# Two layers of a hybrid trunk on one core: TensorE in source order through the mixers, attention units further apart

## The chip, the cores and the metric

The kernel runs on one core of a Trainium2 chip. The metric is device time in microseconds (us) for one execution of the whole program, the median of several runs. The profile is one execution, taken by the hardware profiler.

## The reference, cut to what matters

Two layers are run over 384 tokens: 128 context tokens and 256 denoising tokens, which share the weights. In each layer three token mixers work side by side on one normalised input, and a squared-ReLU MLP follows.

```python
def _layer(x, cond, P, l, ctx=None, tabs=None):
    ...
    h = _rms(x, P['norm1_g'][l]) * (1 + sc1) + sh1
    proj = h @ P['w_in'][l]
    u_conv, dq, dk, dv, cq, ckv, kpe, gl = jnp.split(proj, _split_points(), axis=-1)
    o_conv = _conv_module(u_conv, ...)          # depthwise convolution, 31 taps, 512 channels
    q = _rms(dq...); k = _rms(dk...)            # differential attention, 4 heads
    qm = _rms((rms(cq) @ P['w_uq'][l]), ...)    # latent attention, 8 heads
    km, vm = _mla_expand(ckv, kpe, P['w_ukv'][l], ...)
    ...
    od = _rms(_diff_attend(q, k, v, lam), P['diff_subln'][l]) * (1 - lam_init)
    o_diff = od.reshape(b, s, DIFF_W) @ P['w_diff_out'][l]
    o_mla = _mla_attend(qm, km, vm).reshape(b, s, MLA_W) @ P['w_mla_out'][l]
    gates = jax.nn.sigmoid(gl).reshape(b, s, N_BRANCH, D_MODEL)
    merged = gates[..., 0, :] * o_conv + gates[..., 1, :] * o_diff + gates[..., 2, :] * o_mla
    x = x + g1 * (merged @ P['w_out'][l])
    h = _rms(x, P['norm2_g'][l]) * (1 + sc2) + sh2
    x = x + g2 * (jnp.square(jax.nn.relu(h @ P['w_up'][l])) @ P['w_down'][l])
```

## The kernel before, in words

**Dense products.** Activations lie with channels on the 128 partitions and the 384 tokens along the columns. A product with a weight matrix goes in pieces of 128x1024 weights. SyncE's queue loads a piece (`raw`, L182), ScalarE rounds it into `wh` (L197), VectorE makes the rest `wl = wr - wh` (L198), and TensorE multiplies three times (`passes`, L204 to L206). This is the bulk of TensorE's work; such rows are called dense rows here. There are four buffers for `wr` and `wh` and three for `wl`.

**The mixers.** `mixers` runs three generators together through `weave` (L253). `dense` is the main one: projections to queries, keys and values (`qkv`), the compressed projections (`cproj`), the inputs of the convolution (`conv_in`), the expansions of the latent attention (`mla_q`, `mla_kv`), the gates and the output projections of the branches. Each of its steps reports how much TensorE work it was (1 is three dense rows of 384 columns). `chains` and `attention` are the sides. When a side yields a number it sleeps until that much dense work has been written out; these numbers stand in the table `W`. When it yields a name it sleeps until that flag is set. `tick` and `after` do the same for the delayed second half of a modulation unit (`mod_unit`, L360), the two transposes of L375.

**Attention.** `diff_attention` handles two heads (`c` is 0 or 1) in six units, `mla_attention` four heads (`g` is 0 or 1) in six units. A unit is: scores on TensorE (L753, L759); maxima on VectorE (L754, L760), their product with the scale (L762); exponentials on ScalarE (L766); on VectorE the normalisation, which is L810 to L812 in differential attention, and L967 and two rows of L969 (one for each head) in latent attention; then TensorE transposes the weights (L774 or L981), ScalarE copies them, and TensorE multiplies with the values (L821 or L996).

**The convolution** runs on VectorE: for each of four channel blocks 30 rows of L1071 on tile `z` (120 rows in a layer) and L349, which adds the squares up. `conv` (L1062) is written in the source only shortly before the last branch, but it depends only on `u` and on free `z` buffers. The sum of squares goes to TensorE (three products with ones, L327 with tile `z`), in `conv_norm`, after the first fourth of the output projection of latent attention.

**What sets the order.** The program is recorded in source order. A scheduler then decides the order on each engine: it takes the earliest recorded instruction that its own model thinks ready, and fills an engine that it thinks idle with later ones. That is how the rows of L1071 come between the attention's rows on VectorE, hundreds of rows ahead of their place in the source. The order that it finds is then fixed: on the chip each engine runs its own list from first to last, and waits at each entry for what that needs. `manual_schedule(engines=...)` makes the named engines keep the order of the source; the other engines are still ordered by the scheduler. Before, it is used only in `first_norm` (L1155).

Two places serve as marks below. **Mark A** is L327 with tile `z` in `cproj_norms` (called at L706): right behind the three pairs of L701, in the middle of the input projections. The first row of L1071 in a layer stands within three rows of L1071 of VectorE's answer to it. **Mark B** is L327 with tile `z` in `conv_norm`, near the end of the weave.

Of the kernel before, what the change touches and what calls it, by code (L numbers as in the profile page):

```python
# [36 lines left out]
ZTOK = (0, NP + PAD, 2 * NP + PAD)  # L37
# [93 lines left out]
PIECE = 1024  # L131


W = {"rm": 9, "rx": 8.5, "c0": 3.5, "c1": 2, "mh": 11, "qT": 12.5, "kT": 20, "s": 7, "od": 9, "mq": 7.5, "mk": 11.5, "ms": 9.5, "bc": 11}

NEAR = 2
ENGINES = {mybir.EngineType.PE, mybir.EngineType.Activation, mybir.EngineType.DVE}
# [9 lines left out]
class Body:  # L147
# [99 lines left out]
    def tick(self, w, due=False):  # L247
        for e in self.todo:
            e[0] -= w
        while self.todo and self.todo[0][0] <= (NEAR if due else 0):  # L250
            self.todo.pop(0)[1]()

    def weave(self, main, *sides):  # L253
# [65 lines left out]
        V.scalar_tensor_tensor(y, a, 1.875, y, ALU.add, ALU.mult)  # L319
        return y  # L320

    def rstd_bc(self, acc, toks, ahead=0):

        V = self.V
        st = self.psum("tr")
        for i, o in enumerate(toks):
            self.E.matmul(st[:, i : i + 1], acc[:, o : o + P], self.ones[:, :1], start=True, stop=True)  # L327
        v = self.tl(self.hp, [P, 4], "nwv", 2)
        dg = self.slot("tmp")
        with self.tc.high_priority(ahead):  # L330
            V.tensor_scalar(v[:, :NT], st[:, :NT], EPS, None, op0=ALU.add)
            y = self.rsqrt(v[:, :NT], NT)
            for i in range(NT):
                self.link = V.tensor_scalar(dg[:, i * P : (i + 1) * P], self.ident, y[:, i : i + 1], None,
                                            op0=ALU.mult)
        yield W["bc"]
        bc = self.psum("tr")
        self.E.matmul(bc[:, :T], self.ones, dg, start=True, stop=True)  # L338
        yield 1
        return bc  # L340
# [19 lines left out]
    def mod_unit(self, l, s, p, pool=None):  # L360

        V, E = self.V, self.E
        ps = self.psum("mm" if pool is None or p % 2 else "av")
        for h in range(2):
            w, _, n = self.raw((l, "mod", s, p, h), pool)
            for j in range(4):
                E.matmul(ps[32 * j : 32 * j + 32, :256], self.cond[:, 4 * h + j, :], w[:, j * 256 : j * 256 + 256],
                         start=h == 0, stop=h == 1, tile_position=(0, 32 * j))
        m = self.tl(pool, [P, 256], "m", 5) if pool else self.slot("tmpA", 256)
        self.A.copy(m, ps[:, :256])  # L370

        def rest():
            pt = self.psum("tr")
            for i in range(2):
                E.transpose(pt[:, i * P : i * P + P], m[:, i * P : i * P + P], self.ident)  # L375
            t = self.tl(self.cp, [P, 2, 2], "modt", 2)
            V.tensor_reduce(t, pt[:, : 2 * P].rearrange("p (i j c) -> p i c j", i=2, j=4)[:, :, 0:2, :], AX.X, ALU.add)
            b = self.mod_cols(s, p)
            o = PV["modb"][0]
            V.tensor_tensor(self.modT[l][:, b, :], t, self.pv[l][:, o + b.start : o + b.stop : b.step]  # L380
                            .unsqueeze(2).to_broadcast([P, 2, 2]), ALU.add)

        if pool:
            return rest
        self.after(4, rest)

    def mod_block(self, l, b):

# [399 lines left out]
        V.scalar_tensor_tensor(lo, pt[:, :T], gain, hi.bitcast(F32), ALU.mult, ALU.subtract)  # L788
        return hi, lo

    def diff_attention(self, c):
        V, A, E = self.V, self.A, self.E
        yield f"kT{c}"
        yield f"v{c}"
# [38 lines left out]


        e, last = scores(*units[0]), None
        yield W["s"]
        for i, u in enumerate(units):
            nxt = scores(*units[i + 1]) if i + 1 < len(units) else None
            wT = self.weightsT(e, P if u[0] == 0 else T)
            if last:  # L840
                values(*last)
            e, last = nxt, (*u, wT)
            yield W["s"]
        values(*last)
        y = self.rsqrt(ms, 2 * NT)
        for k in range(2):
# [71 lines left out]
    def mla_T(self, l, g):  # L918

        A, E = self.A, self.E  # L920
        m = self.m[g]
        yield f"mq{g}"
        if g == 1:
            yield "m0"
        yield W["mq"]
        qs = [self.tl(self.ap, [P, 2, T], "qT", 3) for _ in range(2)]
        for hh in range(4):
            pt = self.psum("tr")
            for tt in range(NT):
                E.transpose(pt[0:96, tt * P : tt * P + P], m["x4"][:, tt, hh, :], self.ident)  # L930
            A.activation(qs[hh // 2][0:96, hh % 2, :], pt[0:96, :T], AF.Identity,
                         scale=self.pv[l][0:96, PV["mq"][0] : PV["mq"][1]])
            if hh == 1:
                yield W["mh"]
        self.flags.add(f"mqT{g}")
        yield f"mk{g}"
        yield W["mk"]
        m["pairs"] = []
        for pr in range(2):
            kT = self.tl(self.ap, [P, 2, NK], "kT", 3)  # L940
            for i in range(2):
                hh = 2 * pr + i
                pt = self.psum("tr")
                for tt in range(4):
                    E.transpose(pt[0:96, tt * P : tt * P + P], m["ks"][tt // 2][:, tt % 2, hh, :], self.ident)  # L945
                A.activation(kT[0:96, i, :], pt[0:96, :], AF.Identity,
                             scale=self.pv[l][0:96, PV["mk"][0] : PV["mk"][1]])
            if pr == 0:
                yield W["mh"]
            m["pairs"].append((qs[pr], kT))  # L950
        self.flags.add(f"mkT{g}")

    def mla_attention(self, g):
        V, A, E = self.V, self.A, self.E
        yield f"mkT{g}"
        pairs, vm, qsc = (self.m[g][n] for n in ("pairs", "vm", "qsc"))
# [48 lines left out]


        es, last, done = scores(*units[0]), None, None
        yield W["ms"]
        for i, (pr, tt) in enumerate(units):
            if done is not None:  # L1010
                if g == 1:
# [6 lines left out]
                values(*last)  # L1018
                done = last[0] if last[1] else None
            last = (pr, tt, eT) if tt != 1 else None  # L1020
            yield W["ms"]
        values(*last)
        yield 2
        out(1)
# [51 lines left out]
    def conv_norm(self):  # L1076
        V, A = self.V, self.A
        yield "z"
        bc = yield from self.rstd_bc(self.zacc, ZTOK)
        for b in range(CB):  # L1080
            ch = self.slot("cq", T, F32R)
            cl = self.slot("cq", T, F32R)
            g = self.cgh[:, b : b + 1]
# [111 lines left out]
    def mixers(self, l):  # L1195
# [17 lines left out]
        self.d, self.m = [{}, {}], [{}, {}]  # L1213
        self.od, self.om, self.oc = [], [], []
        m = []
        self.weave(self.dense(l, h, m), self.chains(l), self.attention())
        ap.close()
        self.xs = ExitStack()
        self.xp = self.xs.enter_context(self.tc.tile_pool(name=f"xp{l}", bufs=1))
# [29 lines left out]
    def dense(self, l, h, m):  # L1249
# [21 lines left out]
        for i in range(4):  # L1271
            m += yield from self.gate(l, 1, i, h)
            yield from unit(1)
            if l > 0 and i == 0:
                yield from self.mla_kv(l, 0)
            if i == (1 if l == 0 else 2):
                yield from self.mla_q(l, 1)
            if i == (2 if l == 0 else 3):
                yield from self.mla_kv(l, 1)
        yield "od1"  # L1280
        for i in range(4):
            yield from self.branch_out(l, "od", i, self.od, m[2 * i : 2 * i + 2], None)
            yield from unit(1)
        self.flags.add("od")
        gm = []
# [19 lines left out]
            yield from self.mla_T(l, g)  # L1305
        yield from self.conv_norm()

    def attention(self):
        for c in range(2):
            yield from self.diff_attention(c)  # L1310
        for g in range(2):
            yield from self.mla_attention(g)

    def mlp(self, l):
        V, A = self.V, self.A
# [152 lines left out]
```

## Time and profile before

| | |
|---|---|
| median of 3 runs | 1357.85 us (1356.96 to 1357.92) |
| the profiled execution: its time, its span | 1356.93 us, 1355.2 us |
| TensorE products busy (records of matmuls) | 1330.5 us, 98% of the span, x8096 |
| TensorE weight loads busy | 1256.8 us, 93% |
| VectorE busy | 1067.6 us, 79%, x2549 |
| ScalarE busy | 684.9 us, 51% |
| mean granted TensorE clock over the span | 0.999 |
| layer 1's mixers, mark A to mark B | 825.57 to 984.52 us from the start |

Busy time is the time in which at least one record of the engine runs. TensorE's records overlap: consecutive dense rows of 384 columns start 0.17 us apart and each record is about 0.33 us long, so TensorE's work is better read from starts than from lengths. A wait shows as idle time in front of a row, with the row that ended it.

### The profile page before, as it was taken

The numbers are of one execution on the slowest core, as the hardware profiler recorded it, in microseconds if no ns is written. First come the engines' busy times: TensorE is split into PE (matmuls) and PEld (weight loads), VectorE is DVE, ScalarE is ACT, GpSimd is POOL, SyncE is SP. The second block draws the span as 40 slices with busy tenths as digits, with TensorE's granted clock in tenths as the row PEclk, the third lists the DMA queues.
The fourth block names the chain that finished last, engine by engine and source line by source line (L and its number), as shares of the span: only waits on it lengthen the run. The fifth ranks groups of instructions, "written<-read, shape, count | busy, mean of one in ns | idle before, by whom it ended". The sixth has DMA issues, their size and how long they took to land.

```text
span 1355.2 us, 21851 instructions
## 1 busy us (share of the span) xinstructions
PE 1330.5 (98%) x8096; PEld 1256.8 (93%) x8096; DVE 1067.6 (79%) x2549; ACT 684.9 (51%) x1297; POOL 16.7 (1%) x34
## 2 busy tenths in 40 slices
PE   5999999999999999999999999999999999999998
PEld 3989887789999999999999989878899999999998
DVE  6777999994998999975568789999999897435532
ACT  4555656453544662276335566565444466326621
POOL 0000000000000000000000000000000000000000
PEclk9999999999999999999999999999999999999999
DMA  9533344355574667754444333222358454333341
GB/s 367 180 92 113 109 156 147 127 209 194 162 255 128 206 217 247 250 169 125 148 148 141 90 95 109 84 91 82 124 177 256 142 190 151 125 125 126 125 148 54
DMA packets 62683, 209.46 MB, mean 155 GB/s; under 512 B 7840, under 2 KB 13600, under 8 KB 62320
## 3 DMA queue, kind: packets, MB, share of 16 engines
q1 hardware_dynamic: 56304, 196.93, 44.8%
q0 software_dynamic: 1808, 6.63, 1.5%
q10 hardware_dynamic: 4464, 4.50, 0.9%
q8 instruction: 64, 1.05, 0.3%
q14 instruction: 43, 0.35, 0.1%
HBM read 203.54 MB, written 4.49 MB: 154 GB/s over the span
## 4 chain that ended last, share of the span: by engine, by line
PE 74%; DVE 2%; ACT 1%; issue 0%; DVEq 0%
PE mm L204 15%; PE mm L206 15%; PE mm L205 15%; PE sc L204 8%; PE sc L206 8%; PE sc L205 8%; PE sc L759 1%; PE av L996 1%; PE tr L981 0%; PE av L821 0%; PE tr L338 0%; PE tr L945 0%; PE tr L327 0%; DVE wl L198 0%; DVE nm L760 0%; PE tr L774 0%
## 5 line engine op out<-in xcount | busy, mean ns | idle before, releaser
L197 ACT CAST wh<-wr 128x1024 fp32r<-128x1024 f32 (+3 forms) x280 | 290.0, 1036 | 333.8 <-PE mm L205 165.8
L198 DVE TENSOR_TENSOR wl<-wr,wh 128x1024 fp32r<-128x1024 f32 (+3 forms) x280 | 336.6, 1203 | 143.9 <-PE mm L206 51.6
L204 PE MATMUL mm<-h,wh 128*128 128x384 f32 x848 | 289.6, 341 | 0.5 <-ACT wh L197 0.5
L206 PE MATMUL mm<-h,wl 128*128 128x384 f32 x848 | 285.3, 336 | 0.5 <-DVE wl L198 0.5
L205 PE MATMUL mm<-h,wh 128*128 128x384 f32 x592 | 200.2, 338 | 0.5 <-DVE h L440 0.5
L204 PEld LDWEIGHTS mm<-h,wh 128*128 128x128 f32 x848 | 159.5, 188 | 5.8 <-issue 2.1
L206 PEld LDWEIGHTS mm<-h,wl 128*128 128x128 f32 x848 | 159.5, 188 | 1.8 <-DVE wl L198 1.0
L1071 DVE SCALAR_TENSOR_TENSOR z<-u,dwh,z 128x399 f32<-128x399 f32 x240 | 147.3, 628 | 0.5
L395 DVE SCALAR_TENSOR_TENSOR ot<-wm,srow 128x1024 bf16<-128x1024 f32 x112 | 136.6, 1220 | 4.0 <-DMA wm<-modwT 3.6
L205 PEld LDWEIGHTS mm<-h,wh 128*128 128x128 f32 x592 | 111.5, 188 | 1.6 <-DVE h L440 0.8
L204 PE MATMUL sc<-h,wh 128*128 128x384 f32 x336 | 112.5, 335 | 0.0
L206 PE MATMUL sc<-h,wl 128*128 128x384 f32 x336 | 112.4, 335 | 0.0
L205 PE MATMUL mm<-o,wh 128*128 128x384 f32 x320 | 107.8, 337 | 0.0
L204 PE MATMUL mm<-x,wh 128*128 128x386 f32 x288 | 98.1, 341 | 0.0
L206 PE MATMUL mm<-x,wl 128*128 128x386 f32 x288 | 97.5, 339 | 0.0
L205 PE MATMUL mm<-x,wh 128*128 128x386 f32 x288 | 97.5, 338 | 0.0
L204 PE MATMUL sc<-x,wh 128*128 128x386 f32 x272 | 92.5, 340 | 0.0
L206 PE MATMUL sc<-x,wl 128*128 128x386 f32 x272 | 92.1, 338 | 0.0
L205 PE MATMUL sc<-x,wh 128*128 128x386 f32 x272 | 92.1, 338 | 0.0
L1349 ACT ACTIVATE tmp<-tmp 128x128 f32<-128x128 f32 (+1 forms) x128 | 51.6, 449 | 69.2 <-DVE tmp L1347 69.0
L204 PE MATMUL mm<-wh,h 128*128 128x256 f32 (+1 forms) x288 | 83.8, 291 | 0.0
L206 PE MATMUL mm<-wh,h 128*128 128x256 f32 (+1 forms) x288 | 82.2, 286 | 0.0
(271 smaller groups left out, 2612.5 us busy)
## 6 DMA issues: line engine op xcount, KB each, us to landing
wr<-wts SPq DMA_DIRECT2D x306, 512.0 KB, 3.5
wm<-modwT SPq DMA_DIRECT2D x56, 512.0 KB, 4.4
srow<-condrow POOLq DMA_DIRECT2D x2, 1024.0 KB, 8.7
wr<-wts SPq DMA_DIRECT2D x4, 432.0 KB, 3.4
G<-xT SPq DMA_DIRECT2D x8, 192.0 KB, 4.3
wr<-wts SPq DMA_DIRECT2D x4, 384.0 KB, 3.1
G<-xT POOLq DMA_DIRECT2D x8, 192.0 KB, 3.3
xd<-G ACTq DMA_DIRECT2D x8, 192.0 KB, 2.6
```

What stands on the lines that cost most here:

```text
L197: self.A.copy(hi[:, :n], w[:, :n])
L198: self.V.tensor_tensor(lo[:, :n], w[:, :n], hi[:, :n].bitcast(F32), ALU.subtract)
L204: self.E.matmul(ps, ah, bh, start=start, stop=False)
L205: self.E.matmul(ps, ah, bl, start=False, stop=False)
L206: self.E.matmul(ps, al, bh, start=False, stop=stop)
L395: V.scalar_tensor_tensor(j, w, 0.5, self.srow[:, c, :], ALU.mult, ALU.mult, accum_out=self.modT[l][:, b, c : c + 1])
L759: E.matmul(sc[:, :n], q[c][:, qs], k[c][:, ks], start=True, stop=True)
L996: E.matmul(av[64 * i : 64 * i + 64, q0 : q0 + w], vm[:, (j + 1) if tt else 0, hv : hv + 64], eT[i][:, j * w : j * w + w], start=j == 0, st ...
L1071: self.V.scalar_tensor_tensor(z[b], self.u[:, b, k : k + ZW], self.dw[:, b * CK + k : b * CK + k + 1], z[b], ALU.mult, ALU.add)
L1349: A.activation(r[:, s:e], r[:, s:e], AF.Relu, bias=r[:, T + c : T + c + 1])
```

## The change

`mixers` records the weave under `manual_schedule` for TensorE. So within the weave TensorE runs exactly what the source writes, in that order; VectorE, ScalarE and GpSimd are still ordered by the scheduler. Most sleeping times in `W` are longer, some by layer: units of differential attention 10.2 and 9.2 instead of 7, of latent attention 10.5 and 7.6 instead of 9.5, the keys of latent attention 20 instead of 11.5, the transposes of outputs 14 instead of 9. `mla_kv` of the second group moves from among the gates to the output projections of differential attention. The second half of a modulation unit is due after 14 instead of 4.

```diff
-W = {"rm": 9, "rx": 8.5, "c0": 3.5, "c1": 2, "mh": 11, "qT": 12.5, "kT": 20, "s": 7, "od": 9, "mq": 7.5, "mk": 11.5, "ms": 9.5, "bc": 11}
+W = {"rm": 9, "rx": 8.5, "c0": 3.5, "c1": 2, "mh": 3, "qT": 12.5, "kT": 20, "s": (10.2, 9.2), "od": 14, "mq": (14, 1), "mk": 20, "ms": (10.5, 7.6), "bc": 11, "zc": 16}
...
-        while self.todo and self.todo[0][0] <= (NEAR if due else 0):
+        while self.todo and self.todo[0][0] <= (7 if due else 0):
...
-        yield W["bc"]
+        yield W[wait]
...
-        self.after(4, rest)
+        self.after(14, rest)
...
-        yield W["s"]
+        yield W["s"][l]
...
-        bc = yield from self.rstd_bc(self.zacc, ZTOK)
+        bc = yield from self.rstd_bc(self.zacc, ZTOK, wait="zc")
...
-        self.weave(self.dense(l, h, m), self.chains(l), self.attention())
+        with self.tc.manual_schedule(engines={mybir.EngineType.PE}):
+            self.weave(self.dense(l, h, m), self.chains(l), self.attention(l))
...
-            if i == (2 if l == 0 else 3):
-                yield from self.mla_kv(l, 1)
         yield "od1"
         for i in range(4):
             yield from self.branch_out(l, "od", i, self.od, m[2 * i : 2 * i + 2], None)
+            if i == l:
+                yield from self.mla_kv(l, 1)
```

How the instructions move, at two places of layer 1. The first is TensorE at mark A. Tile `sc` holds scores, `e` the weights of a unit, `z` a sum of squares, `mm` dense products. Before:

```order
L204 MATMUL mm_9427<-h_8135,wh_9431 128x384
L205 MATMUL mm_9427<-h_8136,wh_9431 128x384
L206 MATMUL mm_9427<-h_8135,wl_9432 128x384
L701 MATMUL tr_9474<-ones_99,z_9093 128x1 x3
L327 MATMUL tr_9480<-ones_99,z_9094 128x1 x3
L204 MATMUL mm_9428<-h_8108,wh_9431 128x384
L205 MATMUL mm_9428<-h_8109,wh_9431 128x384
L206 MATMUL mm_9428<-h_8108,wl_9432 128x384
```

And now:

```order
L204 MATMUL mm_9359<-h_8138,wh_9363 128x384
L205 MATMUL mm_9359<-h_8139,wh_9363 128x384
L206 MATMUL mm_9359<-h_8138,wl_9364 128x384
L701 MATMUL tr_9379<-ones_99,z_9056 128x1 x3
L327 MATMUL tr_9385<-ones_99,z_9057 128x1 x3
L759 MATMUL sc_9410<-kT_9069,qT_8829 128x128
L759 MATMUL sc_9413<-kT_9069,qT_8829 128x128
L774 MATMUL tr_9425<-ident_94,e_9328 128x128
```

The scores behind the mark belong to the second unit of the second half of differential attention, the transpose to its first. Before, the scores of five of those six units stood ahead of the mark; now one does. The same holds in layer 0.

The second place is VectorE late in layer 1's latent attention, second group (`e` the weights, `mr` their factors, `nm` maxima, the rows of L1071 the convolution, `wl` the rest of a weight piece, L349 the last sum of squares). Before, from the sixth and last unit of the group on:

```order
L967 RECIPROCAL mr_11038<-ms_2330_11025 128x2
L1071 SCALAR_TENSOR_TENSOR z_11171<-u_102,dwh_7853,z_11171 128x399
L969 TENSOR_SCALAR e_11034<-e_11034,mr_11038 128x384
L969 TENSOR_SCALAR e_11036<-e_11036,mr_11038 128x384
L198 TENSOR_TENSOR wl_11312<-wr_11309,wh_11311 128x1024
L1071 SCALAR_TENSOR_TENSOR z_11171<-u_102,dwh_7853,z_11171 128x399 x6
L198 TENSOR_TENSOR wl_11348<-wr_11345,wh_11347 128x1024
L1071 SCALAR_TENSOR_TENSOR z_11171<-u_102,dwh_7853,z_11171 128x399 x3
L1002 TENSOR_TENSOR o_11143<-av_11042,o_11142 128x384
L1071 SCALAR_TENSOR_TENSOR z_11171<-u_102,dwh_7853,z_11171 128x399 x3
L198 TENSOR_TENSOR wl_11408<-wr_11405,wh_11407 128x1024
L1071 SCALAR_TENSOR_TENSOR z_11171<-u_102,dwh_7853,z_11171 128x399
```

And now, from the third unit of the group on:

```order
L967 RECIPROCAL mr_10882<-ms_2287_10869 128x2
L969 TENSOR_SCALAR e_10878<-e_10878,mr_10882 128x384
L969 TENSOR_SCALAR e_10880<-e_10880,mr_10882 128x384
L349 TENSOR_TENSOR z_11177<-z_11177,tmpA_11309 128x399
L754 TENSOR_REDUCE nm_10927<-sc_10928 128x2
L762 TENSOR_TENSOR nm_10927<-nm_10927,qsc_10266 128x2
L198 TENSOR_TENSOR wl_11092<-wr_11089,wh_11091 128x1024
L967 RECIPROCAL mr_10937<-ms_2300_10926 128x2
L969 TENSOR_SCALAR e_10933<-e_10933,mr_10937 128x128
L969 TENSOR_SCALAR e_10935<-e_10935,mr_10937 128x128
L760 TENSOR_REDUCE nm_10986<-sc_10987 128x1
L760 TENSOR_REDUCE nm_10986<-sc_10990 128x1
```

Before, 13 rows of the convolution come after the group's last unit; now all 120 are over before its third unit, and no row of L1071 follows.

## Rows read from the trace of the kernel before

**Rows 1.** The page: busy time, share of the span, instructions of each engine
```profile
PE 1330.5 (98%) x8096; PEld 1256.8 (93%) x8096; DVE 1067.6 (79%) x2549; ACT 684.9 (51%) x1297; POOL 16.7 (1%) x34
```

**Rows 2.** Windows: us, busy us PE, PEld, DVE, ACT, POOL; granted clock; DMA share, GB/s
```profile
77.70:145.90 68.20, 67.44 (x457) 59.80 (x457) 52.69 (x163) 43.24 (x108) 0.00 (x0) 1.00 0.29 92
145.90:334.30 188.40, 185.27 (x1186) 156.47 (x1184) 163.46 (x467) 98.91 (x215) 1.10 (x2) 1.00 0.48 164
756.60:824.80 68.20, 67.43 (x457) 59.78 (x456) 52.65 (x162) 43.23 (x108) 0.00 (x0) 1.00 0.31 92
824.80:984.70 159.90, 157.87 (x922) 140.01 (x921) 155.58 (x416) 91.19 (x200) 0.55 (x1) 1.00 0.32 103
```

**Rows 3.** Waits of VectorE, layer 1, 824.8 to 984.7 us
```profile
DVE wl L198 <- PE mm L206: 1.6, 5, 0.6
...
DVE oms L592 <- ACT tmpA L591: 0.2, 1, 0.2
```

**Rows 4.** Waits of VectorE, layer 0, 145.9 to 334.3 us
```profile
DVE wl L198 <- ACT wh L197: 6.8, 4, 3.9
```

**Rows 5.** Waits of TensorE, whole span: what waited, for what, us, times, longest
```profile
PE tr L375 <- ACT tmpA L370: 2.1, 1, 2.1
...
PE tr L774 <- DVE e L812: 1.3, 2, 0.6
```

**Rows 6.** VectorE in time, layer 1, third unit of the second latent group
```profile
943.26 1.01 DVE L760 TENSOR_REDUCE nm<-sc 128x1 f32<-128x384 f32 x2
...
945.81 1.23 DVE L198 TENSOR_TENSOR wl<-wr,wh 128x1024 fp32r<-128x1024 f32 x1 [0.38 <-PE mm L206]
946.95 1.18 DVE L1071 SCALAR_TENSOR_TENSOR z<-u,dwh,z 128x399 f32<-128x399 f32 x2
948.04 0.16 DVE L967 RECIPROCAL mr<-ms 128x2 f32<-128x2 f32 x1
...
948.68 0.74 DVE L969 TENSOR_SCALAR e<-e,mr 128x384 f32<-128x384 f32 x2
```

**Rows 7.** TensorE in time, the transposes of the same unit
```profile
949.24 0.85 PE L981 MATMUL tr<-ident,e 128*128 128x128 f32 x6
```

**Rows 8.** Layer 0, second unit of the second latent group: TensorE's transposes
```profile
268.05 0.55 PE L981 MATMUL tr<-ident,e 128*128 128x128 f32 x3 [0.25 <-DVE e L969]
```

**Rows 9.** Chain of waits, 821 to 824 us: a dense row, then one attention unit
```profile
821.21 0.17 PE mm L205
...
821.56 0.84 PE sc L759 x4
822.40 0.48 PE tr L774 x3
822.88 0.67 PE av L821 x6
```

**Rows 10.** TensorE in time, marks A and B of both layers: start us, us
```profile
146.63 0.81 PE L327 MATMUL tr<-ones,z 128*128 128x1 f32 x6
...
334.13 0.72 PE L327 MATMUL tr<-ones,z 128*128 128x1 f32 x6
...
825.57 0.81 PE L327 MATMUL tr<-ones,z 128*128 128x1 f32 x6
...
984.52 0.72 PE L327 MATMUL tr<-ones,z 128*128 128x1 f32 x6
```

**Rows 11.** VectorE in time: the normalisation of one differential unit
```profile
820.62 0.16 DVE L810 RECIPROCAL ra<-s 128x1 f32<-128x1 f32 x1 [0.49 <-ACT e L766]
...
821.07 0.62 DVE L812 SCALAR_TENSOR_TENSOR e<-e,ra,e 128x384 f32<-128x384 f32 x1
```

**Rows 12.** Groups of TensorE: a modulation unit's products (busy us, records)
```profile
L367 PE MATMUL mm<-wr,cond 128*32 128x256 f32 x256 | 19.4, 402 | 0.9 <-DMA wr<-wts 0.9
```

**Rows 13.** Windows near the start; the column behind POOL is the granted clock
```profile
20.00:23.30 3.30, 1.96 (x20) 0.79 (x20) 1.61 (x6) 2.27 (x5) 0.00 (x0) 1.00 1.02 420
23.30:26.80 3.50, 3.00 (x10) 2.54 (x10) 3.20 (x7) 0.89 (x2) 0.00 (x0) 0.51 1.03 424
```

More of the change, by code (lines that the diff above doesn't have):

```diff
@@ L320, in rsqrt, with rstd_bc @@
         return y
-    def rstd_bc(self, acc, toks, ahead=0):
+    def rstd_bc(self, acc, toks, ahead=0, wait="bc"):
         V = self.V
@@ L789, in to_fm, with diff_attention @@
         return hi, lo
-    def diff_attention(self, c):
+    def diff_attention(self, l, c):
         V, A, E = self.V, self.A, self.E
@@ L842, in diff_attention @@
             e, last = nxt, (*u, wT)
-            yield W["s"]
+            yield W["s"][l]
         values(*last)
@@ L924, in mla_T @@
             yield "m0"
-        yield W["mq"]
+        yield W["mq"][g]
         qs = [self.tl(self.ap, [P, 2, T], "qT", 3) for _ in range(2)]
@@ L951, in mla_T, with mla_attention @@
         self.flags.add(f"mkT{g}")
-    def mla_attention(self, g):
+    def mla_attention(self, l, g):
         V, A, E = self.V, self.A, self.E
@@ L1007, in mla_attention @@
         es, last, done = scores(*units[0]), None, None
-        yield W["ms"]
+        yield W["ms"][l]
         for i, (pr, tt) in enumerate(units):
@@ L1020, in mla_attention @@
             last = (pr, tt, eT) if tt != 1 else None
-            yield W["ms"]
+            yield W["ms"][l]
         values(*last)
@@ L1306, in chains, with attention @@
         yield from self.conv_norm()
-    def attention(self):
+    def attention(self, l):
         for c in range(2):
-            yield from self.diff_attention(c)
+            yield from self.diff_attention(l, c)
         for g in range(2):
-            yield from self.mla_attention(g)
+            yield from self.mla_attention(l, g)
     def mlp(self, l):
```

## The prediction

> **What bounds the kernel now.** The page first [rows 1]: TensorE has a record running in 98% of the span, VectorE in 79%. That makes it a TensorE kernel, but both are averages, and the change touches the mixers alone, so I read the mixers by stretches, cut at mark A [rows 2]. Ahead of mark A VectorE is busy 52.7 of 68.2 us in both layers: there is room. Behind it, where the convolution starts, it is busy 155.6 of 159.9 us in layer 1 and 163.5 of 188.4 in layer 0. Then VectorE's waits. In layer 1 behind mark A there are five groups from 1.6 to 0.2 us, 3.0 together [rows 3]: VectorE runs through its list there practically without a pause. In layer 0 it also waits 6.8 us for pieces that ScalarE rounds late [rows 4]. TensorE's own waits in the mixers look small, from 2.1 us down [rows 5].
>
> So in layer 1, and less so in layer 0, there are two full engines side by side. Who leads is seen at one unit. In layer 1 VectorE starts the two rows of L969 that finish the third unit of the second latent group at 948.68 [rows 6]; the first is done after some 0.4 us, and TensorE starts that unit's transposes at 949.24 [rows 7]. In layer 0 TensorE waits 0.25 us in front of the transposes of the second unit for the same line [rows 8]. TensorE arrives within a few tenths of VectorE: the old order on VectorE just fits TensorE's pace. What matters is then how much work each engine has between mark A and such a unit, in either order.
>
> **What the change does to TensorE alone.** No product goes and none comes. A differential unit in one go takes 0.84 us of scores, 0.48 of three transposes (0.16 each) and 0.67 of six value records (0.22 for a pair) [rows 9]. By the order, three score pairs on 384 keys and one on 128, eight transposes and five value pairs cross mark A in each layer: 3 x 0.84 + 0.42 + 8 x 0.16 + 5 x 0.22 = 5.3 us. So mark A comes 5.3 us earlier and the stretch behind it gets 5.3 longer. Counting TensorE's rows at their start-to-start paces (0.17 for a dense row of 384, 0.11 for a plain transpose, and so on) I get 66.2 us for the first stretch of a layer, and 179.1 and 153.7 from mark A to mark B, of 68.2 [rows 2] and of 187.5 and 159.0 us [rows 10]: TensorE loses 2.0, 8.4, 2.0 and 5.3, together 17.7 us. That is all a better order of TensorE could return. I take 1.0 us of each 2.0 ahead of mark A as won, since units there get more room.
>
> **What it does to VectorE.** VectorE is not held to the source; the scheduler ordered it anew around the slower TensorE that it saw, and filled with convolution. I count VectorE's rows from its answer to mark A (L331) to the L969 row of one unit, old order against new, with the times from one start to the next of [rows 6]: L1071 1.09/2 = 0.545 us, L198 1.14, L760 0.47 (half of the pair's 1.01, less the overlap with the row behind); one differential unit's L810 to L812 0.93, which is 0.45 from the first start to the last and 0.48 of the last's 0.62 [rows 11].
>
> Layer 1, third unit of the second latent group: 35 more rows of L1071 (84 to 119) = 19.1; 8 more L760 = 3.7; three differential normalisations = 2.7; one L198 = 1.1; small rows 1.1. Sum **27.7 us** more. TensorE has, up to the same unit, 21 more dense rows (3.6 us, at 0.17 [rows 9]) and the 5.3: about 9 us. VectorE was even with it; now it is some 19 us late.
>
> Layer 0, second unit of the second latent group: 33 more L1071 (86 to 119) = 18.0; 8 L760 = 3.7; four normalisations = 3.7; three L198 = 3.4; five gate rows (L1114, taken like L760) = 2.3; some 30 small rows, among them layer constants that moved, = 3.0. Sum **34.1 us**. TensorE has 57 more dense rows (9.7), the 5.3 and two modulation units (1.4 each: 19.4/16 us of products [rows 12] and two transposes of 0.1): about 18 us, so VectorE is some 16 us late.
>
> TensorE now runs its list strictly. Behind a transpose that waits for its L969 row stand all later dense rows, and ScalarE's copies, the values and the next scores hang on it. The wait can no longer be filled.
>
> **The sum, mark A to mark B.** Layer 1: the transposes started 949.24 - 825.57 = 123.7 us behind mark A [rows 7, 10]; now 123.7 + 27.7 = 151.4. From there to mark B it was 984.52 - 949.24 = 35.3; 21 dense rows fewer (-3.6) and one small score pair more (+0.4) leave 32.1. Together 183.5 against 159.0: +24.5. Mark A comes 5.3 + 1.0 earlier: **+18.2 us**.
>
> Layer 0: 268.05 - 146.63 = 121.4 [rows 8, 10], plus 34.1 = 155.5. The rest was 334.13 - 268.05 = 66.1; 57 dense rows fewer (-9.7), two modulation units (-2.8), one score pair (+0.4), the 2.1 us wait of L375 gone (its second half is due later; -2.1) and some 1.0 of other waits: 50.9. Together 206.4 against 187.5, +18.9, less 6.3: +12.6. About 5 us of VectorE's wait for ScalarE's pieces [rows 4] lie ahead of that unit; with VectorE the late engine the rounding may be ready in time. Without them +7.6. I take the middle, **+10 us**.
>
> Edits with no price: the moved `mla_kv` and its weight piece (one load more or less late among SP's; transfers take 29 to 48% of the DMA engines' time in these stretches, the last column but one of [rows 2]); the later second halves of modulation units, whose results are needed hundreds of us later; `W["zc"]`, the longer sleep in `conv_norm` ahead of the broadcast behind mark B, where some 43 dense rows gave cover already. If VectorE's cover for the last went, the few us of `conv_norm` would come on top. Nothing behind mark B moves.
>
> 1356.93 + 18.2 + 10 = 1385.1 for the profiled execution; the median of the runs is 0.9 above it. I give **1385 us**, slower by 2.0%. Bounds of the terms: layer 0 +6.3 to +12.6, layer 1 +16.2 (if 2.0 more of the old losses vanish) to +18.2, and on top what a late TensorE does to VectorE: its gate rows and maxima wait for TensorE in turn, which the trace does not show; from 0 to the 6.8 us of the largest such row [rows 4].
>
> **Rivals.**
>
> *TensorE keeps its pace (9%).* The convolution rows that moved ahead lie in pauses of VectorE that open only because TensorE is ahead, so no L969 row is late; the 17.7 us come back and it ends at 1340, or at 1349 if half of it does. For it: TensorE's waits on VectorE in the old trace are tiny [rows 5]. Against: VectorE pauses 3.0 us in 159.9 [rows 3]; 35 rows of 0.545 us don't fit. It decides at some 5 us: if VectorE reaches that unit less than 5 us late in each layer, the gains ahead of mark A pay for it.
>
> *A wash (4%).* Layer 0 wins its 8.4 and 2.0, since its VectorE has 25 us to spare in all [rows 2], and layer 1 loses half of the 18: within 3 us of 1358.
>
> *The clock falls too (15%).* At the start there are 3.3 us in which TensorE works 1.96, and in the next 3.5 the granted clock is 0.51, the 1.2 GHz level; ten products take those 3.5 us, 0.35 each instead of 0.17 [rows 13]. Were lateness to pile up in waits of 2 to 4 us, say at the keys of each latent group (four places), each could cost some 1.7 us, 7 in all: 1392. Against: most waits would be about one us. The Trainium skill ("TensorE: Matmul & The Clock Gate", section on HAM oscillation) says that an idle TensorE falls back to half its clock and that a kernel which waits at each step pays for it again and again. By it this rival would be the rule; the mixers of this trace have no wait long enough to tell.
>
> *Forecast (72%)*: late by VectorE's list, at full clock.
>
> **The numbers.** A measurement of this kernel tells about 0.2% (2.7 us) from no change. Slower: forecast and falling clock, 87%; same 4%; faster 9%. The range for 8 in 10 leaves out the first two rivals (13%) and some 5% above. Below it takes in half of layer 1's and the low end of layer 0's term (9 + 6 = 15, less what I may have wrong in the 5.3: 1366); above, 12.6 + 18.2 + 6.8 + the clock's 7 = 44.6 would be 1402, not all of which comes at once: 1398.
>
> **What would show it.** TensorE's waits for L969 and L812 in front of L981 and L774 grow from 2 us to over 20, about a third of it in layer 0; mark A in layer 1 lies at some 158.95 + 24 us before mark B; the last row of L1071 in layer 1 ends more than 25 us ahead of mark B, and VectorE then idles; TensorE's busy share falls to 96 or 97%. A first stretch of 62 us confirms the small term. I am wrong in the mechanism if mark A to mark B in layer 1 stays under 165 us, or if TensorE waits mainly for ScalarE or for weight pieces; wrong in size if the waits for VectorE come out over 35 us.

## The result and the profile after

The changed kernel takes 1398.34 us, median of four runs (1397.82 to 1401.50), against 1357.79: a ratio of 1.0299, 95% interval 1.0286 to 1.0313. It is slower by 40.5 us. The forecast was 1385, and its range ended at 1398. The profiled execution took 1398.51 us with a span of 1396.7. The page, as in [rows 1]:

```profile
PE 1338.3 (96%) x8096; PEld 1264.9 (91%) x8096; DVE 1068.4 (76%) x2549; ACT 687.7 (49%) x1297; POOL 16.7 (1%) x34
```

The work is the same on every engine; only the shares fell. TensorE in time, marks A and B of both layers, as in [rows 10]:

```profile
145.16 0.58 PE L327 MATMUL tr<-ones,z 128*128 128x1 f32 x4
...
347.18 0.61 PE L327 MATMUL tr<-ones,z 128*128 128x1 f32 x5
...
835.45 0.70 PE L327 MATMUL tr<-ones,z 128*128 128x1 f32 x5
...
1026.22 0.61 PE L327 MATMUL tr<-ones,z 128*128 128x1 f32 x5
```

A third place, S, is the row L205 in `first_norm` in front of which TensorE is idle for 0.48 us. Before, then in the changed kernel:

```profile
41.90 0.44 PE L205 MATMUL mm<-h,wh 128*128 128x384 f32 x1 [0.48 <-DVE h L440]
```

```profile
43.27 0.44 PE L205 MATMUL mm<-h,wh 128*128 128x384 f32 x1 [0.48 <-DVE h L440]
```

Up to S the rows of TensorE, VectorE and ScalarE are the same in the same order in every trace of this case, and still S comes anywhere from 41.0 to 44.6 us. So I count what differs ahead of S as no effect of an edit, in a column of its own. Differences of these starts, beside those of before and of the runs that follow, tell where the time went (us; the last column runs from mark B of layer 1 to the end):

| | to S | S to A, layer 0 | A to B, layer 0 | B to A, layer 1 | A to B, layer 1 | rest |
|---|---|---|---|---|---|---|
| before | 41.9 | 104.7 | 187.5 | 491.4 | 159.0 | 370.6 |
| changed | 43.3 | 101.9 | 202.0 | 488.3 | 190.8 | 370.4 |
| e1 order alone | 44.0 | 110.5 | 225.5 | 498.4 | 188.6 | 372.5 |
| e2 table alone | 41.2 | 98.1 | 190.1 | 484.6 | 169.4 | 365.6 |
| e5 no convolution | 41.0 | 103.3 | 192.6 | 486.8 | 168.9 | 370.5 |
| e6 spread | 43.0 | 101.8 | 201.6 | 488.3 | 186.1 | 370.5 |
| e7 filled waits | 41.6 | 101.9 | 201.9 | 488.3 | 189.4 | 370.4 |
| e12 precedence | 41.6 | 98.4 | 201.3 | 485.2 | 187.9 | 370.4 |
| e9 both | 44.6 | 98.5 | 195.6 | 485.2 | 181.8 | 370.4 |
| e13 keys too | 41.1 | 98.4 | 194.9 | 485.2 | 178.9 | 370.4 |
| e14 no convolution, precedence | 41.1 | 98.5 | 190.3 | 485.2 | 170.0 | 370.5 |

The change lost 14.5 us behind mark A of layer 0 and 31.8 behind that of layer 1, and won 2.8 and 3.2 ahead of them; 1.4 us more went by ahead of S. TensorE's waits over the whole span, as in [rows 5]:

```profile
PE tr L945 <- DVE tok L912: 11.1, 4, 3.7
...
PE tr L774 <- DVE e L812: 9.5, 5, 3.4
PE tr L981 <- DVE e L969: 8.2, 8, 2.0
```

So it waits mainly for three rows of VectorE: the last one in making the keys of latent attention (L912), and the normalisations of the two kinds of units. Before, the one for L812 was 1.3 us. Windows, with the columns of [rows 2]: first one of the old trace, from mark A of layer 1 to the transposes of the third unit of the second latent group.

```profile
825.57:949.24 123.67, 121.64 (x705) 107.31 (x704) 121.06 (x351) 72.84 (x163) 0.00 (x0) 1.00 0.29 91
```

The changed kernel: both stretches ahead of mark A, then layer 1 from mark A to that same unit, then on to mark B.

```profile
76.96:145.16 68.20, 64.54 (x447) 60.61 (x446) 45.63 (x135) 38.56 (x88) 0.00 (x0) 0.97 0.31 100
...
767.25:835.45 68.20, 65.46 (x454) 61.61 (x452) 47.76 (x143) 39.65 (x92) 0.00 (x0) 0.97 0.33 96
835.45:994.03 158.58, 139.33 (x755) 120.01 (x755) 149.56 (x411) 82.82 (x185) 0.00 (x0) 0.94 0.24 78
994.03:1026.22 32.19, 32.19 (x193) 28.49 (x194) 14.60 (x29) 15.26 (x34) 0.55 (x1) 1.00 0.39 140
```

To that unit VectorE has 28.5 us more work than before (149.56 less 121.06), and it pauses 9.0 us in place of 2.6. TensorE's granted clock is 0.94 there. Behind that unit TensorE is busy without a gap, and VectorE works 14.6 of 32.2 us. VectorE's waits up to that unit, the counterpart of [rows 3]:

```profile
DVE nm L760 <- PE sc L759: 2.8, 5, 0.7
DVE nm L754 <- PE sc L753: 1.5, 2, 1.2
DVE wl L198 <- PE mm L206: 1.5, 5, 0.7
```

The pauses are new ones: VectorE now waits for scores, which stand behind waiting transposes in TensorE's list. There the two engines delay each other in turn. Not so in layer 0, from mark A to the transposes of the second unit of the second latent group (before, then changed):

```profile
146.63:268.05 121.42, 120.65 (x766) 100.23 (x766) 114.86 (x353) 68.26 (x158) 0.55 (x1) 1.00 0.41 136
```

```profile
145.16:295.28 150.12, 136.72 (x891) 112.89 (x890) 146.73 (x440) 79.42 (x185) 0.56 (x1) 1.00 0.42 137
```

VectorE has 31.9 us more work up to that unit, but its pauses shrank, from 6.6 to 3.4 us.

What a unit looks like inside: VectorE at that third unit, whose scores TensorE gave at 987.36 to 988.74.

```profile
988.21 0.56 DVE L760 TENSOR_REDUCE nm<-sc 128x1 f32<-128x384 f32 x1
988.68 0.62 DVE L1071 SCALAR_TENSOR_TENSOR z<-u,dwh,z 128x399 f32<-128x399 f32 x1
989.22 0.55 DVE L760 TENSOR_REDUCE nm<-sc 128x1 f32<-128x384 f32 x1
989.69 0.62 DVE L1071 SCALAR_TENSOR_TENSOR z<-u,dwh,z 128x399 f32<-128x399 f32 x1
990.49 1.23 DVE L198 TENSOR_TENSOR wl<-wr,wh 128x1024 fp32r<-128x1024 f32 x1 [0.17 <-PE mm L206]
991.63 0.15 DVE L762 TENSOR_TENSOR nm<-nm,qsc 128x2 f32<-128x2 f32 x1
991.70 1.30 DVE L1071 SCALAR_TENSOR_TENSOR z<-u,dwh,z 128x399 f32<-128x399 f32 x2
993.27 0.17 DVE L967 RECIPROCAL mr<-ms 128x2 f32<-128x2 f32 x1 [0.27 <-ACT e L766]
993.47 0.75 DVE L969 TENSOR_SCALAR e<-e,mr 128x384 f32<-128x384 f32 x2
```

From the first maximum to L969 it takes 5.3 us. Between the unit's own rows stand four rows of the convolution and a weight piece. The row of 0.15 us that ScalarE's exponentials need (L762) comes 1.9 us behind the second maximum. TensorE has 21 dense rows in the meantime, and then waits 0.98 us. The profile puts that wait down to L348 of ScalarE, which ends in the same tenth; the transposes start 0.56 us behind the start of L969, as they did before [rows 6, 7], so I count it as a wait for L969.

The same holds where VectorE has time to spare, ahead of mark A of layer 0. There ScalarE ended the exponentials of a differential unit at 104.0:

```profile
103.74 0.96 DVE L634 TENSOR_TENSOR tok<-tok,nwy 128x768 f32<-128x768 f32 x1
104.62 1.22 DVE L198 TENSOR_TENSOR wl<-wr,wh 128x1024 fp32r<-128x1024 f32 x1
105.75 0.42 DVE L636 TENSOR_TENSOR tok<-tok,row 128x256 f32<-128x256 f32 x1
...
107.90 1.22 DVE L198 TENSOR_TENSOR wl<-wr,wh 128x1024 fp32r<-128x1024 f32 x1
109.04 0.41 DVE L585 TENSOR_TENSOR tok<-tok,tmp 128x256 f32<-128x256 f32 x1
109.37 0.15 DVE L810 RECIPROCAL ra<-s 128x1 f32<-128x1 f32 x1
...
110.43 0.60 DVE L812 SCALAR_TENSOR_TENSOR e<-e,ra,e 128x384 f32<-128x384 f32 x1
```

And TensorE:

```profile
111.18 0.66 PE L774 MATMUL tr<-ident,e 128*128 128x128 f32 x2 [3.42 <-DVE e L812]
```

L810 could start at 104 and starts at 109.4, behind rows that make the next keys and two weight pieces. TensorE's old list had dense rows where it now waits 3.4 us.

### The profile page after: what moved, and what is told of

It is laid out like the page before. It is cut to its first block, busy times and chain, and to the rows that moved or that the text cites. A ratio compares the mean times of both kernels' runs of the same rounds, so it can differ in the third digit from the quotient of the medians.

```text
span 1396.7 us, 21854 instructions
## 1 busy us (share of the span) xinstructions
PE 1338.3 (96%) x8096; PEld 1264.9 (91%) x8096; DVE 1068.4 (76%) x2549; ACT 687.7 (49%) x1297; POOL 16.7 (1%) x34
## 4 chain that ended last, share of the span: by engine, by line
PE 83%; DVE 11%; ACT 2%; DMA 2%; issue 1%; SPq 0%; DVEq 0%
PE mm L204 17%; PE mm L206 16%; PE mm L205 16%; PE sc L204 8%; PE sc L206 8%; PE sc L205 8%; DVE z L1071 3%; DVE wl L198 3%; PE sc L759 2%; DMA wr<-wts 1%; PE av L996 1%; PE tr L981 1%; ACT e L766 1%; PE av L821 1%; ACT wh L197 1%
## 5 line engine op out<-in xcount | busy, mean ns | idle before, releaser
L205 PE MATMUL mm<-h,wh 128*128 128x384 f32 x592 | 199.9, 338 | 0.5 <-DVE h L440 0.5
L1071 DVE SCALAR_TENSOR_TENSOR z<-u,dwh,z 128x399 f32<-128x399 f32 x240 | 146.9, 627 | 0.7
L205 PEld LDWEIGHTS mm<-h,wh 128*128 128x128 f32 x592 | 112.4, 190 | 1.2 <-DVE h L440 0.8
L205 PE MATMUL mm<-o,wh 128*128 128x384 f32 x320 | 107.0, 334 | 0.0
L204 PE MATMUL mm<-x,wh 128*128 128x386 f32 x288 | 98.1, 341 | 0.0
L205 PE MATMUL mm<-x,wh 128*128 128x386 f32 x288 | 97.5, 338 | 0.0
L205 PE MATMUL sc<-x,wh 128*128 128x386 f32 x272 | 92.1, 339 | 0.0
```

What stands on the lines that cost most here:

```text
L204: self.E.matmul(ps, ah, bh, start=start, stop=False)
L205: self.E.matmul(ps, ah, bl, start=False, stop=False)
L1071: self.V.scalar_tensor_tensor(z[b], self.u[:, b, k : k + ZW], self.dw[:, b * CK + k : b * CK + k + 1], z[b], ALU.mult, ALU.add)
```

## The experiments

Each is compared with the kernel before on the same chip (its median was 1357.6 to 1359.2 there).

### e1 and e2: the order and the table apart

e1 is the kernel before with the fixed order alone:

```diff
-        self.weave(self.dense(l, h, m), self.chains(l), self.attention())
+        with self.tc.manual_schedule(engines={mybir.EngineType.PE}):
+            self.weave(self.dense(l, h, m), self.chains(l), self.attention())
```

> The kernel before with one edit: TensorE in source order through the mixers; the table of sleeping times and the place of mla_kv stay old. Theory A (the fixed order costs: TensorE waits where VectorE's list, filled with convolution, is late): it is slower than the changed kernel, since the old short sleeping times leave less room. Adding up the durations of the rows of the trace before along the new lists, each wait kept, gives 60 us over before, so 1418 us, and up to 1430 if the clock falls in the waits. Theory B (the table costs: longer sleeping times move attention behind mark A): within 5 us of before, 1353 to 1363.

Measured: 1442.78 us, ratio 1.0624 (1.0603 to 1.0645), 13 us above the upper end.

e2 is the changed kernel without the fixed order:

```diff
-        with self.tc.manual_schedule(engines={mybir.EngineType.PE}):
-            self.weave(self.dense(l, h, m), self.chains(l), self.attention(l))
+        self.weave(self.dense(l, h, m), self.chains(l), self.attention(l))
```

> The changed kernel with TensorE left to the scheduler; the new table and the moved mla_kv stay. Theory A: within 4 us of before, 1354 to 1362, with TensorE's waits in the mixers under 1 us each and no fall of the clock there, though attention crosses mark A as in the changed kernel. Theory B: most of the 40 us remain, 1390 to 1400.

Measured: 1351.54 us, ratio 0.9957 (0.9940 to 0.9973): faster than both kernels. Its longest wait in the mixers is 1.1 us, and the clock stays at 1.00. Its windows ahead of mark A and behind it, layer 1:

```profile
745.70:813.91 68.21, 67.32 (x480) 63.22 (x478) 50.65 (x150) 40.54 (x95) 0.00 (x0) 1.00 0.34 99
813.91:983.27 169.36, 169.21 (x980) 148.38 (x979) 164.72 (x444) 99.03 (x219) 0.55 (x1) 1.00 0.30 105
```

TensorE is busy 169.21 of 169.36 us. So the fixed order costs, 47 us on the new table and 85 on the old one; the table wins 7 without it, and 44 with it. In e2, too, attention crosses mark A: layer 0's mark A comes 6.6 us sooner behind S than before, and layer 1 has the 10 us more behind it (5 of which it gets back behind mark B).

### e3, e4, e5: less convolution on VectorE

e3 and e4 leave out half of the taps in the changed kernel and in the one before:

```diff
-            for k in range(1, CK):
+            for k in range(1, 1 + CK // 2):
```

> The changed kernel with 15 of 31 taps of the convolution left out (60 rows of L1071 fewer in a layer, 33 us of VectorE). It leaves out that part of the convolution. Theory A1 (VectorE's convolution ahead of the attention is all of the loss): the waits go, 1340 to 1355. Theory A2 (the convolution is about half; the other half is the fixed order itself, with TensorE waiting for rows that VectorE has behind weight pieces and waits of its own): 1372 to 1381, by adding up the lists. Theory B or a loss that has nothing to do with VectorE: 1390 or more.

> Control: the kernel before with the same 15 taps left out. All theories: VectorE is relieved, but TensorE leads, so little is won, 1350 to 1356 us. The loss of the change without half of the convolution is e3 less e4: 0 by A1, 17 to 25 by A2, 40 by B.

Measured: e3 1384.56 us (1.0195, 1.0166 to 1.0225), e4 1359.14 (1.0015, 1.0003 to 1.0027). The loss without half of the convolution is 25 us. Theory A1 falls. e3 lies between the bands of A2 and B, and the difference of 25 is the upper end of A2. e4 is 3 us above its band: less work for VectorE wins nothing in the kernel before.

e5 leaves out all rows of L1071:

```diff
-            for k in range(1, CK):
+            for k in range(1, 1):
```

> The changed kernel with all of L1071 left out (one tap of 31 stays, L1068; the rest of the convolution is not computed), 65 us of VectorE less in a layer. Leaving out half gave 14 us back of 40. Theory A (what makes the fixed order dear is the load on VectorE between TensorE's scores and its transposes): the rest goes too, 1345 to 1362, and the clock no longer falls behind mark A. Theory A2 (the fixed order costs by itself, whatever VectorE has to do): 1370 or more.

Measured: 1364.89 us (1.0056, 1.0039 to 1.0073), between the two bands. Of 40.5 us 33.5 are gone; the second half of the convolution is worth 20, the first 14, a split that is good to a few us, since the two runs of e3 lie 6 us apart. The clock still falls, once ahead of mark A of layer 0 and once behind that of layer 1. e5's waits, with L969 at 1.6 in place of 8.2 and L912 no longer among the first:

```profile
PE tr L774 <- DVE e L812: 8.3, 4, 3.4
...
PE tr L981 <- DVE e L969: 1.6, 2, 1.4
```

What stays is the kind of wait that was seen at 111.18, in which no convolution takes part.

### e6, e12, e9: the order of VectorE's list, at equal work

e6 ties each row of the convolution behind the normalisation of a unit (`um` collects these rows, `CAPS` counts how many rows of L1071 may precede each):

```diff
+                r = 30 * b + k - 1
+                u = [w for w, n in zip(self.um, CAPS[l]) if n <= r]
+                with self.tc.issue_after(u[-1].ins) if u else ExitStack():
                     self.V.scalar_tensor_tensor(z[b], self.u[:, b, k : k + ZW],
```

> The changed kernel with the rows of L1071 tied behind the normalisations of the units, so that they spread evenly from mark A to the last unit (in layer 1, 102 rows instead of 120 ahead of the third unit of the second latent group). Same work. If the order of the convolution is the main loss, as in the prediction (27.7 us of rows, most of them convolution, too early): 1378 or less. If the amount of VectorE's work behind mark A is it, in whichever order: 7 us back by adding up the lists, 1386 to 1396.

Measured: 1392.52 us (1.0254, 1.0232 to 1.0277), 6 us back, in the second band. How far the edit reaches matters here. In layer 0, 119 rows of L1071 stood ahead of the second unit of the second latent group (L967) in the changed kernel and 88 before; in e6 it is 91, so the order of before is almost back, and mark A to mark B became 0.4 us shorter. In layer 1, ahead of the third unit, it is 102 (120 changed, 87 before), about half of the way, for 4.7 us.

e12 gives a unit's rows precedence over other rows that are ready; so for L754, L760, L762, L810 to L812, and here:

```diff
-            V.reciprocal(r, s1)
-            for i in range(2):
-                V.tensor_scalar(es[i][:, :n], es[i][:, :n], r[:, i : i + 1], None, op0=ALU.mult)
+            with self.tc.high_priority(1000):
+                V.reciprocal(r, s1)
+                for i in range(2):
+                    V.tensor_scalar(es[i][:, :n], es[i][:, :n], r[:, i : i + 1], None, op0=ALU.mult)
```

> The changed kernel with the precedence of the attention units' rows alone. By adding up the lists 6 us less than the changed kernel, 1389 to 1394, with the waits of TensorE ahead of mark A (3.4 us in layer 0, 2.5 in layer 1, for L812) gone and the clock there at 1.0; if such a wait has another cause than the rows ahead of L810 on VectorE, they stay.

Measured: 1388.20 us (1.0213, 1.0194 to 1.0233), 10 us back, 1 more than the band. The waits for L812 ahead of both marks A are gone, and the clock there is 1.00; the marks come 3.4 us sooner behind S and 3.1 us sooner behind mark B. The stretches from S to mark A of layer 0, and from the L327 with tile `z` ahead of mark A of layer 1 to that mark, in the changed kernel and then in e12:

```profile
43.27:145.16 101.89, 98.23 (x707) 93.94 (x708) 73.25 (x231) 54.99 (x120) 2.53 (x4) 0.98 0.36 117
718.54:835.45 116.91, 113.87 (x797) 109.53 (x796) 90.19 (x267) 65.49 (x145) 2.48 (x4) 0.99 0.37 111
```

```profile
41.63:140.07 98.44, 97.11 (x707) 92.55 (x708) 73.25 (x232) 55.69 (x123) 2.51 (x4) 1.00 0.37 121
712.71:826.50 113.79, 112.52 (x796) 107.97 (x796) 90.32 (x267) 65.57 (x145) 2.49 (x4) 1.00 0.37 114
```

TensorE's idle time fell by 2.3 and 1.8 us (a new wait, of 1.1 and 0.7 us for L617, takes back a part), and its busy time, with the same rows, by 1.1 and 1.4: so much did the half clock cost there.

e9 has both edits, with the convolution spread wider than in e6, up to mark B (94 and 83 rows of L1071 ahead of the two units, in place of 102 and 91):

> The changed kernel, same work, with two edits of VectorE's order only: the rows of an attention unit (L754, L760, L762, L810 to L812, L967, L969) get precedence over other rows that are ready, and the convolution is tied behind the units so that it spreads up to mark B. If the place of a unit's rows behind other rows in VectorE's list is what TensorE waits for: adding up the lists gives 19 us less, so 1375 to 1382. If only the amount of work on VectorE behind mark A counts: no better than the spread alone, 1390 to 1394.

Measured: 1376.44 us (1.0127, 1.0108 to 1.0146), 22 us back, more than the 6 and 10 apart. So neither alone is "the" cause. How much of the difference the wider spread makes was not tried apart. The longest waits left are those for the keys (L950 and L917 are L945 and L912 here):

```profile
PE tr L950 <- DVE tok L917: 10.9, 4, 4.2
...
PE tr L988 <- DVE e L975: 2.9, 6, 1.0
```

The rows that make the keys have no precedence in e9. What stands between them is seen ahead of one of these waits (3.9 us, up to 879.81; L1081 is the convolution, L310 to L320 are steps of `rsqrt`, on 8 columns for the keys, on 6 for other rows):

```profile
876.94 0.63 DVE L1081 SCALAR_TENSOR_TENSOR z<-u,dwh,z 128x399 f32<-128x399 f32 x1
877.48 0.17 DVE L319 TENSOR_TENSOR nwa<-nwa,nwb 128x8 f32<-128x8 f32 x1
877.56 0.16 DVE L314 SCALAR_TENSOR_TENSOR nwy<-nwa,nwy 128x6 f32<-128x6 f32 x1
877.63 0.63 DVE L1081 SCALAR_TENSOR_TENSOR z<-u,dwh,z 128x399 f32<-128x399 f32 x1
878.18 0.16 DVE L320 SCALAR_TENSOR_TENSOR nwy<-nwa,nwy 128x8 f32<-128x8 f32 x1
```

Each small step depends on the one before. The scheduler put a row of the convolution between them, so the steps for the keys start 0.70 us apart (877.48 to 878.18). Where nothing stands between, they start 0.20 us apart (e13, from 874.88 on). A chain of ten steps so grows by some 5 us, an estimate from these two distances.

### e13 and e14: the keys, and what is left without convolution

e13 is e9 with the same precedence for the VectorE rows in `mla_kv`:

> The kernel of e9 (1376.4 us) with precedence on VectorE for the rows that make the keys of latent attention as well (L592 and the rows of rsqrt, L908, L911, L912 in mla_kv). Same work. If the waits at the keys have the same cause: 1364 to 1372, waits for L912 halved. If they come from elsewhere (amount of work on VectorE): 1374 to 1378.

Measured: 1371.21 us (1.0098, 1.0069 to 1.0127), 5 us back, though the intervals of e9 and e13 overlap; in the columns behind S it is 3.7 us. The waits for the keys fell by about as much, to 7.3 us (expected: half of 10.9). Precedence doesn't pull the steps of `rsqrt` together: in e13, too, rows of the convolution stand between most of them. TensorE's waits now (L952 and L919 are L945 and L912, L990 is L981, L778 is L774):

```profile
PE tr L952 <- DVE tok L919: 7.3, 3, 3.2
PE tr L990 <- DVE e L977: 4.4, 6, 2.1
...
PE tr L778 <- DVE e L817: 1.2, 2, 0.7
```

e14 is e5 with precedence for units and keys:

> The kernel of e5 (no rows of L1071; that part of the convolution is not computed; 1364.9 us) with the same precedence for attention units and keys. If the fixed order is free where VectorE answers in time: the 7 us over before go, 1352 to 1359, with no fall of the clock in the mixers. If the fixed order costs by itself: 1362 to 1366.

Measured: 1360.19 us (1.0019, 1.0003 to 1.0035), 5 us less than e5 and just above the band for "free". It is within the 0.2% of before that a measurement can tell. The clock falls once in the mixers, for 3.4 us, 19 us behind mark A of layer 1. The longest waits left there are for ScalarE (L874 and L952 are L870 and L946 here), the clock falls at one of them:

```profile
PE mm L204 <- ACT tok L874: 4.4, 2, 2.6
PE tr L787 <- ACT kT L952: 2.0, 1, 2.0
```

### e7: filling the waits

```diff
+                    if tt == 2 and i == 0 and pr == 0 and (l or g):
+                        for _ in range(24):
+                            E.transpose(pt[:, 2 * P : 3 * P], self.ident, self.ident)
```

> The changed kernel with 24 transposes of the identity (0.11 us each, 2.6 us, into a place that is overwritten right behind) in TensorE's list at three of its longest waits: the keys of the latent groups, layer 0 second group (2.9 us), layer 1 both (3.4 and 3.8 us). VectorE's list hardly changes. If the fall of the clock behind these waits lies on the path: faster, 1388 to 1394, and the granted clock behind them near 1.0. If VectorE is late whatever TensorE's clock: 1397 to 1400. If idle time of TensorE there is not idle at all but needed: slower by up to 8 us.

Measured: 1395.33 us (1.0283, 1.0259 to 1.0308): below the changed kernel by 3 us, but the intervals overlap. The trace decides more. The last of the three places in the changed kernel, then in e7 (granted clock behind POOL):

```profile
962.00:976.00 14.00, 10.26 (x53) 9.74 (x52) 13.24 (x29) 4.51 (x7) 0.00 (x0) 0.76 0.19 65
```

```profile
962.00:976.00 14.00, 12.02 (x85) 11.34 (x84) 13.75 (x32) 5.17 (x12) 0.00 (x0) 1.00 0.23 75
```

The fall is gone there, and the whole stretch from mark A to mark B of layer 1 got 1.3 us shorter, that of layer 0 0.1. VectorE is late there at either clock; the half clock behind mark A of layer 1 costs little: 10.2 us less of it (the fall at the first of layer 1's two places lasts 3.4 us in place of 6.8, that at the second, 6.8 us, is gone) won 1.3. The other 1.6 us of the 3 lie ahead of S, where no run differs in its rows.

### e8, e10, e11: can the table alone be bettered, and what in it wins

e8 puts the second head's normalisation (L969) of e2 on ScalarE:

> The table-alone kernel (1351.5 us) with the second head's normalisation in latent attention (L969) on ScalarE: 12 rows, 4.4 us, off VectorE in each layer. If VectorE's work sets layer 1 behind mark A there (169.4 us in e2 against 159.0 before): 1344 to 1349. If TensorE's order leads: 1350 to 1353.

Measured: 1352.20 us (0.9958, 0.9944 to 0.9971), the same as e2. From mark A to mark B of layer 1 it takes 164.4 us, 5.0 less than e2, and 4.9 more behind mark B: only the mark's place in TensorE's list moved. TensorE leads in e2.

e10 gives e2 the precedence of e9 and a spread like that of e9:

> The table-alone kernel (TensorE left to the scheduler, 1351.5 us) with the same precedence and spread. If the rest of TensorE's losses there are waits for VectorE's rows: 2 to 4 us faster, 1347 to 1350. If TensorE's own order leads: 1350 to 1353.

Measured: 1352.72 us (0.9952, 0.9939 to 0.9964), the same again. The order on VectorE that is worth 22 us to the fixed order is worth nothing where TensorE's rows can be moved.

e11 is the kernel before with the two sleeping times of differential attention alone:

```diff
-"s": 7,
+"s": (10.2, 9.2),
```

> The kernel before with the sleeping times of differential attention alone from the new table (10.2 and 9.2 for 7), TensorE left to the scheduler. If these times are what wins the 6 us of the table (mark A 7 us earlier in each layer): 1350 to 1354, with mark A of layer 0 at 139 to 140 us. If the moved pieces and the later second halves are: 1356 to 1362.

Measured: 1362.49 us (1.0026, 1.0016 to 1.0035), just above the second band. Mark A of layer 0 comes at 141.1, 5.6 us earlier, but from there to mark B it takes 195.2 us, 7.7 more than before. These times alone don't win; which of the others does was not tried.

## Why the prediction was right and wrong

**Direction and place: right.** It had TensorE late by VectorE's list, behind mark A, more in layer 1, with VectorE idle at the end. The last row of L1071 in layer 1 starts 33.9 us ahead of mark B (it said more than 25), and TensorE's share is 96%. One sign was missed: the waits for L969 and L812 came to 17.7 us, not to over 20 (18.7 with the one that the profile puts down to L348), half of it and not a third in layer 0, and the largest group, 11.1 for the keys (L912), the sign did not name.

**The count of VectorE's rows: right in layer 1, too high in layer 0.** In layer 1 it forecast 27.7 us more up to the third unit, measured 28.5 busy. From that unit to mark B it forecast 32.1, and it is 32.2. In layer 0 it forecast 34.1 more up to the second unit, and that unit came 28.7 later: 31.9 busy, less 3.2 of pauses. From there to mark B it forecast 50.9, and it is 51.9. The prediction allowed for about 5 us of waits for ScalarE's pieces ahead of that unit, but misread them: only 2.1 of the 6.8 us of [rows 4] lie ahead of it, and they are 1.0 in the changed kernel. The middle that I took, +16.3 from mark A to mark B, was 1.8 above the measured 14.5, and near for a reason that was half wrong.

**The step that failed: two terms taken at their best.** Of the 13.3 us between 28.2 and 41.5 (the spans) there are

- 7.3 in layer 1 behind mark A (+31.8, not +24.5). The text gave "what a late TensorE does to VectorE" as 0 to 6.8 us and took 0. VectorE's pauses up to the third unit grew by 6.4 (9.0 less 2.6). When TensorE waits, its scores come later, and VectorE pauses for those.
- 6.6 ahead of the two marks A. I took 6.3 us earlier at each, with 1.0 "won, since units there get more room"; it was 2.8 and 3.2. VectorE is idle a quarter of that stretch before, and I read that as room. But one wait of 3.4 and one of 2.5 us, each followed by half clock, took it back. e12, where they are gone, has both marks 6.3 us earlier than before, which was the forecast.
- 1.4 ahead of S, which belongs to the two profiled executions and to no term.
- less 1.8 in layer 0 behind mark A, and 0.2 behind the last mark.

**The named cause: half right.** The prediction put the loss down to convolution rows that come too early. Leaving them out returns 33.5 us, but spreading them only 6, and 0.4 in layer 0, where they were almost all put back. What counts, as far as these runs tell, is that a unit passes VectorE twice, that at each pass any row may stand ahead of it (convolution, weight pieces, the next keys), and that TensorE, once its order is fixed, has nothing else to run. Precedence and spread together return 22, with the keys 27. Against the rest over before (13 us) stand 12.9 us of waits for keys and units in e13 (1.6 before). What bounds the fixed order below that is open. Even without convolution and with precedence (e14) it is 9 us above the table alone, and there its longest waits are for ScalarE.

**The rivals.** "TensorE keeps its pace" came near its milder figure (1349) where the fixed order is left out: e2 takes 1351.5, and the 7 us that it wins lie within the 17.7 that the prediction counted as TensorE's losses. "The clock falls too" came true in what the clock did: it fell at six places in the mixers. It was priced at 7 us; e12 bears out 1.1 and 1.4 ahead of the marks A, and e7 about 1.3 for two of the falls behind them. The Trainium skill ("TensorE: Matmul & The Clock Gate", section on HAM oscillation) has waits paid again and again by a slower clock. The trace agrees that the clock falls at six waits of 2.0 to 3.8 us (one of 2.9 in layer 0 has no fall), and differs in the price behind mark A: there TensorE at half speed ran towards a row that was late anyway.

The Trainium skill ("Perfetto Trace Analysis", section on the most-contended engine) has one optimise the engine with the highest occupancy first. By that it is TensorE in the changed kernel, at 96%, or 91% by weight loads, by which the same section has one judge TensorE's headroom. The trace agrees that the loss shows as TensorE's idle time (58.4 us of the span in place of 24.7), but its source is another engine: taking 110 us of work off VectorE, at 76%, gave 33.5 us (e5), with TensorE's rows untouched.

## What to carry to other kernels

In this kernel, fixing the order of one engine while a scheduler orders the others took away the slack that hid their latency: the fixed engine then needs each answer within the gap that the source leaves, whatever rows stand ahead of it in the other queue. So don't only compare sums of work up to a point; follow one unit through the other engine's list, row by row, and hold the longest such passage against the gap. And test the parts of such a change apart: here the table alone wins 0.4%, and the order that came with it costs 3.5%.

## What was not expected of the hardware

A stretch in which VectorE is a third idle (45.6 of 68.2 us busy ahead of mark A) still gave the longest wait of TensorE in layer 0 (3.4 us), since VectorE's list runs in order: L810 was ready at 104.0 and stood until 109.4 behind rows of other work. And half clock for 6.8 us behind a wait can cost very little: in e7 the granted clock of a 14 us stretch rose from 0.76 to 1.00, and that layer's mixers became 1.3 us shorter.
